# Compression with its weights stationary, and full-width groups for the recurrence's operands, in a two-layer RWKV-7 / sparse-attention trunk

## The chip, the core and the metric

The kernel runs on one core of a Trainium2 chip. Five engines work side by side, each through its own queue in order: TensorE (matmuls and transposes into PSUM), VectorE, ScalarE, GpSimd and SyncE, which issues the DMAs. The metric is the device time of one execution in microseconds.

## The reference

Two layers over 256 tokens of width 2048, batch 1. Each modulates its input, projects it, mixes tokens in two head groups, projects back, normalizes, and applies a squared-ReLU MLP. Two parts of the token mixer matter here.

The recurrence (16 heads of 64) is a generalized delta rule:

```
S = S * w_t[:, :, None, :] + sa[..., None] * (kk_t * a_t)[:, :, None, :] + v_t[..., None] * k_t[:, :, None, :]
return S, jnp.einsum('bhvk,bhk->bhv', S, r_t)
...
o = ((o - mu_o) * lax.rsqrt(var_o + GN_EPS)).reshape(B, T, D_RWKV) * lnx_g + lnx_b
```

The output is centred per head before it is scaled; the kernel centres the values `v` beforehand, which gives the same.

The sparse attention (16 query heads, 4 key/value heads) compresses keys and values: blocks of 32 tokens, every 16 tokens, 15 blocks in all, are flattened to 2048 numbers and put through a small MLP with 256 hidden units.

```
blocks = jnp.transpose(blocks, (0, 3, 1, 2, 4)).reshape(B, G, n_cmp, CMP_BLOCK * N)
return jax.nn.gelu(blocks @ w1) @ w2
```

## The kernel before

Activations lie transposed, features on partitions and the 256 tokens along the free dimension. Every large product is done in three matmuls of a reduced float32 type: the weights arrive by DMA into `wf` (5 buffers, shared with the compression's weights), ScalarE casts them to `wh` (line 226), VectorE makes the remainder `wl` (227), and `mm3` runs `wh*xh + wl*xh + wh*xl` into `acc` (128 stationary columns, 256 moving). `block` does one 128-column output so; its evict step follows. The order on each engine is made by a planner that walks the program with priorities and a cost model, and places other ready work where an instruction would wait. So projection matmuls `acc` stand between the small ones.

The recurrence works on chunks of 64 tokens. `rwkv_a` prepares one pair of heads, 8 pairs in a layer, in two halves of four (`half_in`); it is called 16 times. It makes decay products, normalized keys and, in `bk` (128 partitions = 2 heads x 64 features; 4 chunks x 3 slots x 64 tokens), the scaled operands: slot 0 and 1 for both, and slot 2, a copy of slot 0 for the second head. The matrices `mt` come from `bk` and `UR`; VectorE masks them (543, 544), ScalarE copies parts of them out (547, 549). Then, for each head, four transposes per call turn 64 rows by 128 columns of `bk` into `bkt`, and ScalarE copies `bkt` to `BK` (552 to 555). The centred values: four matmuls take 64 tokens each of `vt` as stationary against the constant `cent` into `vp`, and two ScalarE copies store them in `SV`, the second head on partitions 0 to 63 and the first on 64 to 127 (556 to 560). `bonus` (562) follows. All of `zw`, `za`, `tp`, `rb`, `mt`, `bkt`, `vp` and `bonus` take turns in the two PSUM banks named "a". `rwkv_b` inverts triangular matrices on VectorE, 31 dependent steps in lines 575 and 577; `rwkv_c` runs the chunks one after the other.

`compress` runs twice in a layer (keys, values), after the second and the fourth of the `Kd` projections. `kcp` holds the gathered blocks: 128 partitions, 16 slices of 64 columns (4 heads x 16 blocks). The hidden layer is 16 matmuls with a slice of `kcp` stationary (64 columns) and 256 weight columns moving; they write partitions 0 to 63 and 64 to 127 of `hid` in turn, two partial sums that lines 772 and 773 add. GELU follows on 64 partitions x 256, then two transposes `xt` (781) and a copy bring the hidden units onto partitions for the second layer. The weights come in four DMAs of 512 KB.

In the profile a float32 matmul leaves two records, a transpose one. Nearly all matmuls go through the helper in line 206, so groups are told apart by their tiles.

Of the kernel before, what the change touches and what calls it, by code (L numbers as in the profile page):

```python
# [15 lines left out]
OP = mybir.AluOpType  # L16
# [151 lines left out]
def tile_trunk(tc, ap, outT, dbg=None):  # L168
    nc = tc.nc
    V, A, G, PE, SY = nc.vector, nc.scalar, nc.gpsimd, nc.tensor, nc.sync  # L170
    with ExitStack() as ctx:
# [6 lines left out]
        def st(tag, shape, dt=FT, name=None):  # L178
            if dbg is not None:
                dbg.setdefault("_sz", {})  # L180
                dbg["_sz"][tag] = max(dbg["_sz"].get(tag, 0), int(np.prod(shape[1:])) * 4 * BUFS.get(tag, 1))
            return sb.tile(shape, dt, name=name or tag, tag=tag, bufs=BUFS.get(tag, 1))
# [4 lines left out]
        def mx(th, shape, name="mx"):  # L187
            return psp.tile(shape, FT, name=name, tag="mx" + th, bufs=1 if th in "mn" else 2)
# [10 lines left out]
        ident = cs("ident")  # L199
# [210 lines left out]
        for l in range(NL):  # L410
# [80 lines left out]
            def rwkv_a(pi, p, r, k, H):  # L491
# [48 lines left out]
                for h, (me, ot) in enumerate(halves):  # L540
                    ur, tm, mt = H["UR"][p][h], H["TM"][p][h], mts[h]
                    rm = cs("rmask")
                    V.tensor_mul(ur[ot], mt[ot], rm[ot, None, :].to_broadcast([64, 4, 128]))
                    V.tensor_mul(tm[me, :, 64:128], mt[me, :, 64:128], rm[me, None, 64:128].to_broadcast([64, 4, 64]))
                    for q in range(2):
                        r0 = h * 64 + q * 32
                        A.copy(Dt[r0:r0 + 32, :, p * 4:p * 4 + 4].rearrange("p t c -> p c t"),
                               mt[r0:r0 + 32, :, q * 32:q * 32 + 32])
                    A.copy(tm[h * 64:h * 64 + 32, :, 32:64], mt[h * 64:h * 64 + 32, :, 32:64])
                    tp = mx("a", [128, 4, 64], "bkt")  # L550
                    for c in range(4):
                        PE.transpose(tp[:, c], bk[me, c, h:h + 2].rearrange("p a b -> p (a b)"), ident[me, me])
                    bt = st("BK", [128, 4, 64])
                    H["BK"][p][h] = bt
                    A.copy(bt, tp)
                vp = mx("a", [64, 4, 2, 64], "vp")
                for c in range(4):
                    mm(vp[:, c].rearrange("p a b -> p (a b)"), vt[:, c * 64:c * 64 + 64], cs("cent"))
                A.copy(H["SV"][0][64:128, p], vp[:, :, 0])
                A.copy(H["SV"][1][0:64, p], vp[:, :, 1])  # L560
                bp = mx("a", [128, T], "bonus")
                mm(bp, cs("bones"), sq)
                V.tensor_mul(vt, bp, vt)
# [196 lines left out]

            def compress(kv, kcp):

                hid = mx("n", [128, 256], "hid")
                for q in range(4):
                    w = st("wf", [128, 4, 256], name="cw1")
                    SY.dma_start(w, ap["cw1"][l, kv, q].rearrange("p (a b) -> p a b", a=4))
                    for j in range(4):
                        o = j % 2 * 64
                        mm(hid[o:o + 64], kcp[:, 4 * q + j].rearrange("p g c -> p (g c)"), w[:, j], q * 4 + j < 2, q * 4 + j > 13)
                xr, y = slab(name="xr"), slab(name="gy")  # L770
                xr, y = xr[0:64], y[0:64]
                A.copy(xr, hid[64:128])
                V.tensor_add(xr, xr, hid[0:64])
                A.activation(y, xr, AF.Square)
                V.tensor_scalar(y, y, 0.044715, 1.0, op0=OP.mult, op1=OP.add)
                V.tensor_mul(y, y, xr)
                A.activation(y, y, AF.Tanh, scale=math.sqrt(2.0 / math.pi))
                V.scalar_tensor_tensor(xr, y, 1.0, xr, op0=OP.add, op1=OP.mult)
                xt = mx("n", [128, 2, 64], "xt")
                for b in range(2):  # L780
                    PE.transpose(xt[:, b], xr[:, b * 128:b * 128 + 128], ident[0:64, 0:64])
                x = st("cg1", [128, 2, 64])
                A.copy(x, xt)
                if kv == 0:
                    kp = mx("n", [128, 2, 16], "kp")
                    for g in range(4):
                        for b in range(2):
                            mm(kp[g % 2 * 64:g % 2 * 64 + 64, g // 2], cw2[:, 0, b], x[:, b, g * 16:g * 16 + 16], b == 0, b == 1)
                    for h in range(2):
                        A.mul(kcd[h * 64:h * 64 + 64, :, h], kp[h * 64:h * 64 + 64], 0.5)  # L790
                else:
                    vp = mx("n", [32, 2, 64], "vp2")
                    for gp in range(2):
                        for b in range(2):
                            mm(vp[:, gp], x[:, b, gp * 32:gp * 32 + 32], cw2[:, 1, b], b == 0, b == 1)
                    for h in range(2):
                        A.activation(vcb[:, :, h * 64:h * 64 + 64], vp, AF.Copy, scale=cs("hm")[0:32, h:h + 1])

            Kd = [[None] * 2 for _ in range(2)]
            kcp = compress_in(0)  # L800
# [354 lines left out]
```

## Time and profile before

| | |
|---|---|
| median of 3 runs | 2805.02 us (2801.45 to 2806.73) |
| profiled execution | 2805.57 us, of which the span is 2803.7 us |
| TensorE matmuls | busy 2682.2 us (96%), 22794 records |
| VectorE | busy 2088.5 us (74%) |
| ScalarE | busy 1507.1 us (54%) |
| mean granted TensorE clock | 0.981 of full speed |

The sum of a change is set against the profiled execution. A busy TensorE is not one at its peak: a row's duration holds the time in the pipeline, and neighbouring rows overlap. Where the matmuls are packed, the distance between starts tells what one costs.

### The profile page before, as it was taken

Reading aid. Unit: us, or ns where it says so; the run is one execution under the profiler, and the core shown is the slowest. Engines: PE = TensorE matmul, PEld = TensorE weight load, DVE = VectorE, ACT = ScalarE, POOL = GpSimd, SP = SyncE. Lnnn points to the kernel's source line nnn. Section 1 sums busy time; section 2 is a strip of 40 time slices with the busy share of each in tenths; the row PEclk is TensorE's granted clock in tenths of the full one; section 3 lists DMA queues with packets and bytes.
Section 4 is the critical chain, followed back from the end, with each engine's and each line's share of the span. In section 5 each row is a group of like instructions: output and inputs, shape, how many; then the busy total and the mean of one; then the engine's idle time right before and its main releaser. Section 6 shows DMA issues by size and latency. Waiting matters only on the chain.

```text
span 2803.7 us, 59395 instructions
## 1 busy us (share of the span) xinstructions
PE 2682.2 (96%) x22794; PEld 2450.1 (87%) x22794; DVE 2088.5 (74%) x4710; ACT 1507.1 (54%) x3221; POOL 69.6 (2%) x205
## 2 busy tenths in 40 slices
PE   6999899998999999999999999999999999999997
PEld 4777678756999999999999888887799999999997
DVE  3677868656789788888998786886796566666567
ACT  3344345554585554645557544556567565464555
POOL 0000010000000000000000001000000000000000
PEclk9999999898999999999999999999999999999998
DMA  8986656386579899999986444333466777776664
GB/s 302 320 271 229 239 190 196 121 265 211 171 231 370 316 344 339 338 352 336 342 266 200 140 150 129 120 107 119 157 197 187 235 217 235 231 233 205 195 191 126
DMA packets 206780, 639.63 MB, mean 228 GB/s; under 512 B 23392, under 2 KB 42848, under 8 KB 206496
## 3 DMA queue, kind: packets, MB, share of 16 engines
q1 hardware_dynamic: 206496, 635.83, 68.0%
q8 instruction: 179, 2.93, 0.4%
q14 instruction: 105, 0.86, 0.1%
HBM read 629.45 MB, written 6.29 MB: 227 GB/s over the span
## 4 chain that ended last, share of the span: by engine, by line
PE 78%; DVE 13%; DMA 4%; ACT 3%; issue 2%; SPq 0%; ACTq 0%; POOL 0%; DVEq 0%
PE acc L206 65%; DVE wl L227 4%; PE gv L206 2%; DMA wap<-in_wad 1%; ACT wh L226 1%; PE ot L206 1%; PE pt L896 1%; PE mt L206 1%; DMA wf<-in_win 1%; DVE Tt L577 1%; DVE fs L575 1%; PE va L206 1%; PE vp L206 1%; PE tp L206 0%; PE rb L206 0%
## 5 line engine op out<-in xcount | busy, mean ns | idle before, releaser
L226 ACT CAST wh<-wf 128x512 fp32r<-128x512 f32 x1536 | 946.1, 620 | 859.0 <-PE acc L206 483.4
L227 DVE TENSOR_TENSOR wl<-wf,wh 128x512 fp32r<-128x512 f32 x1536 | 1038.5, 689 | 384.2 <-ACT wh L226 372.8
L206 PE MATMUL acc<-hhi,wh 128*128 128x256 f32 x3456 | 983.5, 285 | 17.1 <-ACT wh L226 8.8
L206 PE MATMUL acc<-hhi,wl 128*128 128x256 f32 x3456 | 972.3, 281 | 8.7 <-DVE wl L227 8.5
L206 PE MATMUL acc<-hlo,wh 128*128 128x256 f32 x3456 | 971.9, 282 | 0.2 <-DVE hlo L407 0.2
L206 PE MATMUL acc<-hi,wh 128*128 128x256 f32 x2560 | 714.8, 279 | 8.1 <-DVE res L1059 3.8
L206 PE MATMUL acc<-lo,wh 128*128 128x256 f32 x2560 | 715.4, 280 | 1.3 <-DVE lo L215 1.3
L206 PE MATMUL acc<-hi,wl 128*128 128x256 f32 x2560 | 714.8, 279 | 0.1
L206 PEld LDWEIGHTS acc<-hhi,wh 128*128 128x128 f32 x3456 | 656.8, 190 | 61.2 <-issue 24.1
L206 PEld LDWEIGHTS acc<-hhi,wl 128*128 128x128 f32 x3456 | 655.7, 190 | 18.2 <-DVE wl L227 12.9
L206 PEld LDWEIGHTS acc<-hlo,wh 128*128 128x128 f32 x3456 | 654.6, 190 | 8.7 <-issue 4.5
L206 PEld LDWEIGHTS acc<-hi,wh 128*128 128x128 f32 x2560 | 484.6, 189 | 10.5 <-ACT hi L214 5.0
L206 PEld LDWEIGHTS acc<-lo,wh 128*128 128x128 f32 x2560 | 483.3, 189 | 3.6 <-DVE lo L215 2.4
L206 PEld LDWEIGHTS acc<-hi,wl 128*128 128x128 f32 x2560 | 484.1, 189 | 1.4 <-issue 0.8
L344 DVE CUSTOM_DVE_ANT_0 wa<-wa,cond,modh 128x1024 f32<-128x1024 f32 x112 | 143.3, 1279 | 0.0
L344 DVE CUSTOM_DVE_ANT_0 wa<-wa,cond,vec 128x1024 f32<-128x1024 f32 x112 | 143.3, 1279 | 0.0
L206 PE MATMUL gv<-wap,cT 128*32 128x512 f32 x640 | 90.6, 639 | 21.7 <-DMA wap<-in_wad 21.4
L1099 DVE TENSOR_TENSOR lo<-relu,hi 128x256 fp32r<-128x256 f32 x128 | 54.1, 425 | 45.5 <-ACT relu L1098 45.3
L288 DVE TENSOR_TENSOR sum<-sum,acc 128x512 f32<-128x512 f32 x70 | 48.1, 687 | 45.8 <-PE acc L206 45.8
L883 ACT ACTIVATE P<-P,tyn 128x128 f32<-128x128 f32 (+1 forms) x128 | 57.3, 448 | 11.8 <-DVE tyn L881 11.1
L1097 ACT ACTIVATE hi<-relu 128x256 fp32r<-128x256 f32 x128 | 53.5, 422 | 3.5
L1098 ACT ACTIVATE relu<-relu 128x256 f32<-128x256 f32 x128 | 53.3, 420 | 3.6
(290 smaller groups left out, 2352.5 us busy)
## 6 DMA issues: line engine op xcount, KB each, us to landing
wf<-in_w SPq DMA_DIRECT2D x512, 512.0 KB, 4.6
wa<-in_wada SPq DMA_DIRECT2D x224, 512.0 KB, 5.6
wf<-in_win SPq DMA_DIRECT2D x192, 512.0 KB, 4.1
wap<-in_wad SPq DMA_DIRECT2D x208, 256.0 KB, 4.7
wf<-in_wout SPq DMA_DIRECT2D x64, 512.0 KB, 4.1
wap<-in_wad SPq DMA_DIRECT2D x56, 512.0 KB, 5.1
cw<-in_cw SPq DMA_DIRECT2D x16, 512.0 KB, 4.1
xin<-in_xT SPq DMA_DIRECT2D x16, 128.0 KB, 5.5
```

What stands on the lines that cost most here:

```text
L206: return PE.matmul(o, l, r, start=start, stop=stop, skip_group_check=True)
L226: A.copy(wh, wf[:, s])
L227: V.tensor_sub(wl, wf[:, s], wh.bitcast(FT))
L288: V.tensor_add(s, s, bank)
L344: V.tensor_tensor_reduce(wa, wa, cb, 0.5, init, OP.mult, OP.add, dst)
L575: V.tensor_mul(x, Mu[:, j + 1:32, j:j + 1].to_broadcast([128, n, w]), Tt[:, j:j + 1, 0:w].to_broadcast([128, n, w]))
L577: V.tensor_sub(Tt[:, j + 1:32, 0:w], Tt[:, j + 1:32, 0:w], x)
L883: A.activation(P[:, h, c:c + n], P[:, h, c:c + n], AF.Exp, bias=m[:, 2 * h + i:2 * h + i + 1], scale=-1.0, accum_out=z[:, 2 * h + i:2 * h ...
L896: PE.transpose(pt[:, h, c * 128:c * 128 + 128], P[:, h, 256 * i + c * 128:256 * i + c * 128 + 128], ident)
L1097: A.activation(hi, t, AF.Square)
L1098: A.activation(t, t, AF.Square)
L1099: gate[0] = V.tensor_sub(lo, t, hi.bitcast(FT)).ins
```

## The change

Three edits. In `rwkv_a`, the two groups of four transposes with 64 rows become one group of four with all 128 rows, both heads at once; the first head's operand is copied out in one piece, the second's in two, with the halves of the partitions exchanged (slot 2 is still made for `mt`). The centred values take 128 tokens a matmul, two matmuls instead of four, and four copies of 64x128 in place of two of 64x256. In `compress` the weights become stationary (128 columns) and the 64 columns of `kcp` move; the hidden units so land on partitions, the two partial sums and their addition, the two transposes and one copy go, and GELU works on 128 partitions x 128.

```diff
-                    tp = mx("a", [128, 4, 64], "bkt")
-                    for c in range(4):
-                        PE.transpose(tp[:, c], bk[me, c, h:h + 2].rearrange("p a b -> p (a b)"), ident[me, me])
-                    bt = st("BK", [128, 4, 64])
-                    H["BK"][p][h] = bt
-                    A.copy(bt, tp)
-                vp = mx("a", [64, 4, 2, 64], "vp")
+                tp = mx("a", [128, 4, 128], "bkt")
                 for c in range(4):
-                    mm(vp[:, c].rearrange("p a b -> p (a b)"), vt[:, c * 64:c * 64 + 64], cs("cent"))
-                A.copy(H["SV"][0][64:128, p], vp[:, :, 0])
-                A.copy(H["SV"][1][0:64, p], vp[:, :, 1])
+                    PE.transpose(tp[:, c], bk[:, c, 0:2].rearrange("p a b -> p (a b)"), ident)
+                H["BK"][p] = [st("BK", [128, 4, 64]) for h in range(2)]
+                A.copy(H["BK"][p][0], tp[:, :, 0:64])
+                for r in (0, 64):
+                    A.copy(H["BK"][p][1][64 - r:128 - r], tp[r:r + 64, :, 64:128])
+
+                vp = mx("a", [128, 2, 2, 64], "vp")
+                for i in range(2):
+                    mm(vp[:, i].rearrange("p a b -> p (a b)"), vt[:, i * 128:i * 128 + 128], cs("cent"))
+                for e in range(2):
+                    for h in range(2):
+                        A.copy(H["SV"][h][64 - h * 64:128 - h * 64, p, e:4:2], vp[e * 64:e * 64 + 64, :, h])
...
-                hid = mx("n", [128, 256], "hid")
+                hid = mx("n", [128, 2, 64], "hid")
...
-                        o = j % 2 * 64
-                        mm(hid[o:o + 64], kcp[:, 4 * q + j].rearrange("p g c -> p (g c)"), w[:, j], q * 4 + j < 2, q * 4 + j > 13)
-                xr, y = slab(name="xr"), slab(name="gy")
-                xr, y = xr[0:64], y[0:64]
-                A.copy(xr, hid[64:128])
-                V.tensor_add(xr, xr, hid[0:64])
+                        for b in range(2):
+                            mm(hid[:, b], w[:, j, b * 128:b * 128 + 128], kcp[:, 4 * q + j].rearrange("p g c -> p (g c)"),
+                               q + j + b == 0, q * 4 + j == 15)
+                xr, y = slab(name="xr")[:, 0:128], slab(name="gy")[:, 0:128]
+                x = st("cg1", [128, 2, 64])
+                A.copy(xr, hid.rearrange("p a b -> p (a b)"))
...
-                V.scalar_tensor_tensor(xr, y, 1.0, xr, op0=OP.add, op1=OP.mult)
-                xt = mx("n", [128, 2, 64], "xt")
-                for b in range(2):
-                    PE.transpose(xt[:, b], xr[:, b * 128:b * 128 + 128], ident[0:64, 0:64])
-                x = st("cg1", [128, 2, 64])
-                A.copy(x, xt)
+                V.scalar_tensor_tensor(x.rearrange("p a b -> p (a b)"), y, 1.0, xr, op0=OP.add, op1=OP.mult)
```

## Rows read from the trace of the kernel before

**Rows 1.** The page's part 4: chain that ended last, shares by engine.
```profile
PE 78%; DVE 13%; DMA 4%; ACT 3%; issue 2%; SPq 0%; ACTq 0%; POOL 0%; DVEq 0%
```
**Rows 2.** Busy time by stretch: length, PE, PEld, DVE, ACT, POOL, clock, DMA share, GB/s.
```profile
1610.00:1630.00 20.00, 19.61 (x151) 17.61 (x150) 15.87 (x48) 11.96 (x27) 0.70 (x4) 1.00 0.36 111
1650.00:1670.00 20.00, 18.71 (x154) 17.61 (x152) 19.22 (x49) 6.58 (x13) 0.00 (x0) 1.00 0.49 158
```
**Rows 3.** TensorE's waits over the span: us in total, times, longest.
```profile
PE bkt L552 <- ACT TM L549: 2.9, 9, 0.6
...
PE hid L206 <- DMA cw<-in_cw: 2.1, 3, 1.6
```
**Rows 4.** Timeline of TensorE, one call in layer 1: start, us, what (stationary, moving).
```profile
1620.24 0.28 PE L206 MATMUL acc<-hlo,wh 128*128 128x256 f32 x1
1620.45 0.46 PE L552 MATMUL bkt<-cst,a 64*128 64x64 f32 x4
...
1621.07 0.28 PE L206 MATMUL acc<-hhi,wl 128*128 128x256 f32 x1
...
1622.35 0.28 PE L206 MATMUL acc<-hhi,wl 128*128 128x256 f32 x1
1622.47 0.28 PE L206 MATMUL acc<-hlo,wh 128*128 128x256 f32 x1
1622.68 1.09 PE L206 MATMUL vp<-cst,vt 128*64 128x128 f32 x8
1623.70 0.39 PE L206 MATMUL acc<-hhi,wh 128*128 128x256 f32 x1
1623.92 0.28 PE L206 MATMUL acc<-hhi,wl 128*128 128x256 f32 x1
1624.04 0.59 PE L206 MATMUL bonus<-a,cst 128*128 128x256 f32 x2
...
1624.69 0.48 PE L206 MATMUL zw<-lx,wa 96*128 96x256 f32 x1
```
**Rows 5.** Timeline of TensorE around four transposes of 128 by 128.
```profile
422.72 0.28 PE L206 MATMUL acc<-hlo,wh 128*128 128x256 f32 x1
422.84 0.60 PE L385 MATMUL gv<-cst,gs 128*128 128x128 f32 x4
423.19 0.37 PE L206 MATMUL acc<-hhi,wh 128*128 128x256 f32 x1
423.40 0.28 PE L206 MATMUL acc<-hhi,wl 128*128 128x256 f32 x1
```
**Rows 6.** Timeline of TensorE: float32 matmuls with 128 stationary columns.
```profile
212.32 0.52 PE L206 MATMUL tp<-cst,a 128*128 128x2 f32 x4
212.71 0.36 PE L206 MATMUL acc<-hhi,wh 128*128 128x256 f32 x1
...
403.17 1.06 PE L206 MATMUL rb<-lx,g 128*128 128x256 f32 x4
```
**Rows 7.** Groups of ScalarE by form: busy us, mean ns of one, idle before.
```profile
L555 ACT COPY BK<-bkt 128x256 f32<-128x256 f32 x32 | 11.8, 373 | 5.0 <-PE bkt L552 4.7
L549 ACT COPY TM<-mt 32x128 f32<-32x128 f32 x32 | 8.2, 256 | 0.5
L560 ACT COPY SV<-vp 64x256 f32<-64x256 f32 x16 | 5.9, 367 | 0.2
```
**Rows 8.** Timeline of ScalarE in the call of rows 4.
```profile
1624.27 0.37 ACT L560 COPY SV<-vp 64x256 f32<-64x256 f32 x1
```
**Rows 9.** Timeline of TensorE: the compression's `hid` matmuls, three of their runs.
```profile
314.59 1.08 PE L206 MATMUL hid<-cw,kcp 128*64 128x256 f32 x8 [1.55 <-DMA cw<-in_cw]
...
1671.92 4.92 PE L206 MATMUL hid<-cw,kcp 128*64 128x256 f32 x26
...
1693.15 3.64 PE L206 MATMUL hid<-cw,kcp 128*64 128x256 f32 x30 [1.02 <-DVE fs L575]
```
**Rows 10.** Busy time by stretch, columns as in rows 2.
```profile
1672.00:1676.00 4.00, 4.00 (x24) 2.33 (x25) 3.34 (x10) 0.43 (x1) 0.00 (x0) 0.58 0.70 245
```

## The prediction

> **What bounds the kernel now.** I read the chain that ended last first: TensorE's matmuls hold 78% of it, VectorE 13%, transfers 4% [rows 1]. So a microsecond of TensorE time is, on average, most of a microsecond of the result. Then the busy time in the stretches of the change: in the first half of layer 1's recurrence TensorE is busy for 19.61 of 20 us, VectorE for 15.87, ScalarE for 11.96; forty microseconds later, while the triangular inverse runs, VectorE has 19.22 and TensorE 18.71 [rows 2]. TensorE is the limit while the operands are made, and two engines are close to it during the compression. Last come TensorE's waits: all transposes `bkt` together waited 2.9 us for ScalarE, and `hid` 2.1 us for its weights [rows 3]. Little is lost in waiting around the edited lines, so what must be counted is how long each matmul group occupies the array. That isn't the duration of a row, since matmuls overlap; it is the distance from the start of one row to the start of the next.
>
> **Transposes of the recurrence's operands.** In the run of projection matmuls, starts are 0.12 us apart (1622.35 to 1622.47). A group of four `bkt` transposes, 64 rows by 128 columns, takes from 1620.24 to 1621.07, 0.83 us with two ordinary steps of 0.12 in it, so 0.59 us; 0.09 of that is on entry (0.21 to its first row instead of 0.12) [rows 4]. There are two groups in each call: 1.18 us. The new group is four transposes of 128 by 128. The trace has just that at `gv`: 422.72 to 423.40 is 0.68, less 0.24, so 0.44 us; entry costs nothing extra there [rows 5]. Gain: 0.74 us a call.
>
> **Centred values.** Eight `vp` records (each float32 matmul leaves two) take 1622.47 to 1623.92, which is 1.45 less 0.24, so 1.21 us, and 1.02 from their start to the next row's, 0.128 a record [rows 4]. Four records with the same 128 moving columns but 128 stationary ones replace them. They are bounded by `tp`, whose records have 128 stationary and 2 moving columns and stand 0.39 / 4 = 0.098 us apart, and by 0.128; full-width records with 256 moving columns last 1.06 us for four (`rb`) and 0.59 for two (`bonus`), 0.235 each, so half as many columns take 0.118 [rows 4, 6]. I take 0.11, between `tp` and `rb`; the 0.128 has a switch in it. So 0.44, and 0.09 for entry and exit as at `gv`: 0.53. Gain 0.68 us, with bounds 0.61 and 0.73. With the transposes it is 1.42 us a call, and there are 16 calls (8 head pairs, 2 layers): **-22.7 us**.
>
> **ScalarE's copies.** `BK` for the second head becomes two copies of 64 partitions instead of one of 128: 0.373 + 2 x 0.367 instead of 2 x 0.373, so +0.36 us. `SV` becomes four copies of 64x128 for two of 64x256. The trace has no 64x128 copy; it lies between 0.256 (32x128) and 0.367 (64x256) [rows 7]. I take 0.256, as the elements along a partition are the same: +0.29 (at most +0.73). Together +0.65 us a call, 10.4 us of ScalarE. What hides it is the 8 us in 20 that ScalarE is idle [rows 2], and projection matmuls that the planner puts between. What it delays is the next call: its first matmul `zw` starts at 1624.69 [rows 4], just after the last `SV` copy, 1624.27 plus 0.37 [rows 8], since `zw` and `vp` draw on the same two banks. Behind a late `zw` in TensorE's queue stand the projection matmuls. Nothing lost in most calls and the whole 0.65 in some: I charge 0.2 a call, **+3 us** (bounds 0 and 10.4; at the upper `SV` price 17).
>
> **Compression.** Before, 8 records of `hid` last 1.08 us and 30 last 3.64, so 22 more are 2.56 us, 0.116 each [rows 9]; 32 make 3.7, and 0.2 for entering and leaving: 3.9 us. After, there are 64 records: 128 stationary columns are loaded for 64 moving ones. Load and moving part overlap in the rows seen, so the load sets the pace: 0.098 (`tp`) to 0.128 (`vp`) [rows 6, 4]. I take 0.11: 7.0 us, +0.1: 7.1, so +3.2. The two `xt` transposes go; by the `bkt` group, 0.59 less two of its four records, some 0.45 us. Net +2.75, four times: **+11.0 us** (bounds +8 and +15). Of this the `hid` matmuls' waits for weights are given back, as a slower group waits less: one quarter of the weights was waited for 1.55 us [rows 9], all together 2.1 [rows 3]. **-2 us**. One VectorE addition, one ScalarE copy less and shorter operations between also fall away, off TensorE; I take nothing for them, though where VectorE is full [rows 2] they may be worth 1 or 2 us. The DMAs are the same 16 transfers in the same place; each buffer is held some 0.8 us longer, which delays the next weight load where transfers are the limit.
>
> The pairs of `hid` now write two 64-column strips of the array, and their 256 columns cost 0.116 us where an `rb` record of 256 costs 0.235 [rows 9, 6]. So the two run side by side, and the edit gives that up. The Trainium skill, TensorEngine Tiling (Array Packing), section When to Use Tiling, advises just the form that is taken away: with 64 or fewer moving columns, swap the operands and tile the columns by two. By that rule alone the edit doubles the compression's array time; by the rows it nearly does, and it is the other two edits that would have to pay for it.
>
> **Sum.** -22.7 + 3 + 11 - 2 = -10.7 us. The profiled execution took 2805.57 us, 0.55 above the median of the runs shown; the sum gives 2794.9, and from the median 2794.3. I forecast 2794 us, its own range 2786 to 2799. A measurement of this kernel can tell about 0.2%, 5.6 us, from no change.
>
> **Rivals.**
> *The freed TensorE time is not the limit.* The projection matmuls that move up need `wl` from VectorE, which is full from 1650 on [rows 2]. If only half of the -22.7 is kept, the sum is -11.3 + 3 + 9, about +1: 2806, no change. For it speaks the nearness of VectorE; against it, the first half, where VectorE has 4 us in 20 to spare. Chance 0.17.
>
> *ScalarE's queue sets the pace of the calls (slower).* Place: `zw` behind the last `SV` copy. A call for which this holds gains nothing on TensorE and ends 0.65 us later, instead of 1.42 earlier. With n such calls the sum is -22.7 + 2.07 n + 9: it turns at 7 of 16 and is slower by over 0.2% from 10; with all 16 it is +19, 2825 us. Rows 8 speak for it, the small waits of rows 3 against it. Chance 0.11.
>
> *The clock falls during the compression (slower).* The granted clock is 0.58 on average from 1672 to 1676 us, so it stood at its lower level, 1.2 GHz, for most of that [rows 10], and 26 records of `hid` take 4.92 us there, 0.19 each [rows 9]. In the new form the moving part fills only half the time of each load. At the lower level 64 records cost 14 us, 7 more. Two of four compressions would end at +3, three at +10, 2815 us, and only from there is it slower by over 0.2%. Against it: the 0.58 is no 0.50, so the clock came back while `hid` ran, and the other groups ran at 0.116 a record. Chance 0.08 for three or four.
>
> *Loads don't overlap.* If the load and the moving part followed each other, a record would cost 0.098 and some 0.06 (a quarter of `rb`'s 0.235), 0.158; 64 make 10.1 instead of 7.0, four times +12.4: about +2, 2807, no change. The rows of `rb` speak against it: with loads as wide, their 0.235 is also what two of `hid`'s side by side give (twice 0.116), whose loads are half as wide; a load of 0.098 in series would show. The Trainium skill, TensorE: Matmul & The Clock Gate, Part 3, says that a weight load overlaps a running matmul only where the row groups differ, which would be this case; Part 2 of that page allows it also for the background buffer. By the first rule the time would be this rival's. Chance 0.05.
>
> **Chances.** The forecast and a larger gain 0.59. Faster 0.61 (with 0.02 of the half-kept case); same 0.22 (the rest of that case, the loads, and ScalarE in 7 to 9 calls); slower 0.17 (ScalarE in ten calls or more, the clock). The range: at the lower end -22.7 - 1, no cost of ScalarE, compression at +8 - 2: -18, and another 5 if a stretch at half clock goes; 2782. At the upper end it takes in the cases without change and the milder slow ones (ScalarE in up to 10 or 11 calls): 2811.
>
> **What would show it.** `bkt` with 64 records of 128x128 instead of 128, one group of about 0.44 us a call; `vp` with 64 records instead of 128, 0.45 from start to next; `hid` with 256 records some 0.11 apart, 7 us a time, at clock 1.00; no `xt`; ScalarE's busy time up by 8 us or so; TensorE still busy for over 19 of 20 us in layer 1's first half, with calls closer together than 19 us. I am wrong if `zw` waits for `SV` on TensorE, if `hid` stands at the lower clock, or if the projection matmuls wait longer for `wl`.

## The result and the profile after

The changed kernel took 2821.62 us, median of 8 runs (2811.86 to 2826.31), beside 2803.98 us for the kernel before in the same session. The ratio is 1.0055, 95% interval [1.0032, 1.0077]: slower, by some 15 us, where 2794 us was forecast. Three of the eight runs took 2812 to 2814 us and five 2821 to 2826 us; the profiled one is of the first three (2811.86 us, span 2810.1 us).

The chain that ended last hardly changed; it shows by itself neither the loss nor where it lies [rows 1]:

```profile
PE 78%; DVE 12%; ACT 5%; DMA 3%; issue 2%; SPq 0%; POOL 0%; ACTq 0%; DVEq 0%
```

The sizes that the prediction gave to the groups of matmuls are there. In TensorE's timeline of a call of layer 1 (the columns of [rows 4]) the four transposes take 0.41 us to the next start, and the four `vp` records 0.46 and 0.09 on leaving (0.21 to the second `acc` for 0.12):

```profile
1575.24 0.28 PE L206 MATMUL acc<-hhi,wh 128*128 128x256 f32 x1
1575.78 0.66 PE L552 MATMUL bkt<-cst,a 128*128 128x128 f32 x4 [0.26 <-ACT TM L549]
1576.19 0.36 PE L206 MATMUL acc<-hhi,wl 128*128 128x256 f32 x1
1576.84 0.71 PE L206 MATMUL vp<-cst,vt 128*128 128x128 f32 x4 [0.28 <-ACT TM L549]
1577.30 0.36 PE L206 MATMUL acc<-hlo,wh 128*128 128x256 f32 x1
1577.51 0.28 PE L206 MATMUL acc<-hhi,wh 128*128 128x256 f32 x1
```

But both groups now begin with a wait, in brackets. Of TensorE's waits over the whole span, that of `vp` for `TM` was 0.9 us, 4 times, before; those of `zw` for `SV` and of `bonus` for `BK` are new, and `hid` waits no longer for its weights but for the gather on VectorE [rows 3]:

```profile
PE vp L206 <- ACT TM L549: 4.4, 11, 0.6
PE bkt L552 <- ACT TM L549: 2.1, 7, 0.4
PE hid L206 <- DVE kcp L761: 2.0, 1, 2.0
PE zw L206 <- ACT SV L563: 1.6, 7, 0.4
PE bonus L206 <- ACT BK L556: 1.0, 3, 0.4
```

The windows say the same: TensorE, busy for 19.61 of 20 us before, is busy for 18.95 now [rows 2]. Of the 1.3 us of array time that a call needs less, 0.7 us in these 20 stand there as idle time. From the first `gp` of layer 1 (transposes ahead of its recurrence) to its first `hid`, a stretch with four of the calls, both kernels need 146.1 us (1521.5 to 1667.6 before, 1514.7 to 1660.8 after), and `zw` follows `zw` at 20.0 us where it was 19.1 and 19.7.

```profile
1610.00:1630.00 20.00, 18.95 (x139) 16.91 (x139) 15.33 (x46) 12.53 (x30) 0.72 (x3) 1.00 0.38 112
...
1684.00:1688.00 4.00, 2.93 (x16) 2.77 (x17) 3.16 (x8) 0.00 (x0) 0.00 (x0) 0.75 0.22 35
1688.00:1692.00 4.00, 4.00 (x21) 4.00 (x20) 3.73 (x11) 1.14 (x2) 0.31 (x1) 0.50 0.67 227
1692.00:1696.00 4.00, 4.00 (x21) 4.00 (x20) 1.55 (x3) 0.00 (x0) 0.00 (x0) 0.50 0.44 131
1696.00:1700.00 4.00, 4.00 (x20) 4.00 (x20) 0.00 (x0) 0.66 (x3) 0.00 (x0) 0.50 0.52 139
```

The last four rows are the second compression of layer 1. From the first `hid` to the first `va` the kernel before needed 122.9 us (1667.6 to 1790.5), the changed one 137.5 (1660.8 to 1798.3); `va` belongs to the sparse attention, behind the compression. These 14.6 us are more than the 6.3 us between the two profiled executions, since the changed one had entered layer 1 6.8 us ahead. Most of that lead, 5.8 us, arose behind layer 0's first `va`, where only one of its eight calls lies, at a mean clock of 0.99 for 0.98, so little of it can come from the edits. The two runs of 56 `hid` records in that layer show how:

```profile
1663.75 6.36 PE L206 MATMUL hid<-kcp,cw 128*128 128x64 f32 x56
...
1685.07 1.08 PE L206 MATMUL hid<-kcp,cw 128*128 128x64 f32 x8 [1.96 <-DVE kcp L761]
...
1686.89 12.04 PE L206 MATMUL hid<-kcp,cw 128*128 128x64 f32 x56
```

The first run takes 0.114 us a record, at full clock. The second comes behind a wait of 1.96 us for the gather, and takes 0.215 a record. TensorE is busy for all of 1688 to 1700, and the granted clock is 0.50, the level of 1.2 GHz, all the while. In the kernel before such a run also began slowly, but the clock was back within some 4 us [rows 9, 10], as its window from 1676 us shows (columns as in rows 2):

```profile
1676.00:1680.00 4.00, 4.00 (x34) 3.54 (x31) 3.12 (x7) 1.90 (x5) 0.21 (x1) 0.99 0.98 299
```

In the kernel before, VectorE was busy for 19.22 of 20 us around the start of the first compression [rows 2]. Here it stands still for much of the slow run, as its own timeline shows:

```profile
1692.29 1.26 DVE L227 TENSOR_TENSOR wl<-wf,wh 128x512 fp32r<-128x512 f32 x2
1702.33 0.69 DVE L227 TENSOR_TENSOR wl<-wf,wh 128x512 fp32r<-128x512 f32 x1 [8.78 <-ACT wh L226]
1703.04 1.00 DVE L588 COPY TM<-O 32x128 f32<-32x128 f32 x6
```

A remainder `wl` waits 8.78 us for its cast `wh`. In ScalarE's queue that cast stands behind the copy `xr`, which itself waits for the last `hid`:

```profile
1698.97 0.27 ACT L776 COPY xr<-hid 128x128 f32<-128x128 f32 x1 [8.17 <-PE hid L206]
...
1701.68 0.62 ACT L226 CAST wh<-wf 128x512 fp32r<-128x512 f32 x1 [2.06 <-issue]
```

It starts when twelve projection matmuls behind `hid` have run; that it waits for the buffer that they free is argued, since the trace names no releaser. Behind `wl` in VectorE's queue stands the result of the triangular inverse (`TM<-O`), on which the recurrence's next matmuls hang. So a slow compression is paid for twice, in its own time and in what it holds up.

ScalarE's new copies came out as costed [rows 7], and its busy time is 1516.3 us, 9.2 more:

```profile
L563 ACT COPY SV<-vp 64x128 f32<-64x128 f32 x64 | 16.7, 260 | 1.0
L556 ACT COPY BK<-bkt 64x256 f32<-64x256 f32 x32 | 11.7, 367 | 0.4
```

### The profile page after: what moved, and what is told of

Its sections match the earlier page's. It is cut to its first block, busy times and chain, and to the rows that moved or that the text cites. A ratio compares the mean times of both kernels' runs of the same rounds, so it can differ in the third digit from the quotient of the medians.

```text
span 2810.1 us, 59434 instructions
## 1 busy us (share of the span) xinstructions
PE 2684.2 (96%) x22786; PEld 2466.5 (88%) x22786; DVE 2088.4 (74%) x4706; ACT 1516.3 (54%) x3265; POOL 71.2 (3%) x205
## 4 chain that ended last, share of the span: by engine, by line
PE 78%; DVE 12%; ACT 5%; DMA 3%; issue 2%; SPq 0%; POOL 0%; ACTq 0%; DVEq 0%
PE acc L206 65%; DVE wl L227 4%; PE gv L206 2%; ACT wh L226 1%; PE hid L206 1%; PE ot L206 1%; DMA wap<-in_wad 1%; PE pt L894 1%; PE mt L206 1%; ACT Dt L547 1%; PE va L206 1%; PE tp L206 1%; PE sc L206 1%; DVE Tt L580 0%; DVE fs L578 0%
## 5 line engine op out<-in xcount | busy, mean ns | idle before, releaser
L881 ACT ACTIVATE P<-P,tyn 128x128 f32<-128x128 f32 (+1 forms) x128 | 57.3, 448 | 13.8 <-DVE tyn L879 12.5
```

What stands on the lines that cost most here:

```text
L881: A.activation(P[:, h, c:c + n], P[:, h, c:c + n], AF.Exp, bias=m[:, 2 * h + i:2 * h + i + 1], scale=-1.0, accum_out=z[:, 2 * h + i:2 * h ...
```

## The experiments

In the table a ratio is to the kernel before, run on the same chip; clock is the mean granted clock over all executions of a kernel, beside that of the kernel before in the same session. A straight line through the 265 executions, each kernel about its own mean, gives 1.5 us for each 0.001 of clock. "Rest" is the difference of the means less that much: it is a rough guide, good to perhaps 3 us.

| kernel | median us | ratio, 95% | clock (before) | rest us |
|---|---|---|---|---|
| recur_only | 2796.34 | 0.9988 [0.9971, 1.0004] | 0.9793 (0.9794) | -4 |
| compress_only | 2816.86 | 1.0060 [1.0042, 1.0077] | 0.9775 (0.9794) | +13 |
| more_scalar | 2801.73 | 1.0000 [0.9987, 1.0013] | 0.9793 (0.9794) | +1 |
| wide_moving | 2800.89 | 1.0010 [0.9994, 1.0025] | 0.9831 (0.9799) | +8 |
| two_kcp | 2821.08 | 1.0077 [1.0051, 1.0102] | 0.9758 (0.9799) | +15 |
| layer0_only | 2805.03 | 1.0022 [1.0005, 1.0038] | 0.9805 (0.9799) | +6 |
| layer1_only | 2816.46 | 1.0050 [1.0031, 1.0070] | 0.9773 (0.9805) | +9 |
| recur_wide | 2806.52 | 1.0050 [1.0032, 1.0068] | 0.9810 (0.9816) | +11 |
| recur_vector | 2797.49 | 0.9997 [0.9982, 1.0013] | 0.9797 (0.9799) | -1 |
| half_array | 2790.85 | 0.9983 [0.9969, 0.9997] | 0.9802 (0.9816) | -7 |
| before_short | 2794.58 | 0.9990 [0.9975, 1.0004] | 0.9802 (0.9816) | -5 |
| recur_short | 2785.51 | 0.9966 [0.9953, 0.9978] | 0.9799 (0.9816) | -13 |
| half_short | 2783.95 | 0.9945 [0.9930, 0.9960] | 0.9812 (0.9805) | -15 |
| recur_two | 2784.06 | 0.9941 [0.9925, 0.9958] | 0.9827 (0.9805) | -13 |
| before_two | 2803.94 | 1.0022 [1.0005, 1.0038] | 0.9767 (0.9803) | 0 |
| recur_two_b | 2784.80 | 0.9957 [0.9942, 0.9972] | 0.9811 (0.9803) | -13 |

The changed kernel itself has a mean clock of 0.9749.

### Which edit

**recur_only**: the two edits of the recurrence, with the compression as before.

> The two recurrence edits without the compression's. If TensorE's array time sets the pace of the calls (my sum), this is 20 to 23 us faster than before, less some 3: about 2785 us. If the chain of a call through ScalarE sets it, the freed array time is worth nothing and each of the 16 calls ends 0 to 0.65 us later: 0 to +10 us, 2804 to 2814, and zw starts stand 19.7 to 20.3 us apart in the first half of layer 1 instead of 19.1 to 19.7.

**compress_only**: the compression's edit, with the recurrence as before.

> The compression's edit without the recurrence's. If only array time counts, +9 to +11 us, about 2814. If the clock falls in layer 1's second compression as it does in the changed kernel, and VectorE's queue stands behind the longer hid, +12 to +25 us, and hid's records are 0.21 us apart there. If recurrence edits and compression only hurt together, under +5 us.

**more_scalar**: the kernel before, with the copies `SV` made twice.

```diff
-                A.copy(H["SV"][0][64:128, p], vp[:, :, 0])
-                A.copy(H["SV"][1][0:64, p], vp[:, :, 1])
+                for _ in range(2):
+                    A.copy(H["SV"][0][64:128, p], vp[:, :, 0])
+                    A.copy(H["SV"][1][0:64, p], vp[:, :, 1])
```

> The kernel before with its two SV copies made twice, so 0.73 us more of ScalarE in each of 16 calls and nothing else. If ScalarE's queue sets the pace of the calls, most of 16 x 0.73 = 11.7 us is seen: +6 to +12 us, and zw starts stand 0.5 to 0.7 us further apart. If TensorE sets it and ScalarE's idle time covers the copies: 0 to +2 us.

**after_again**: the changed kernel once more.

> The changed kernel unaltered, for a second profile. Its times lie at 2812 to 2814 us and at 2819 to 2826. If the clock makes that difference, this profile has the same order of work and other stretches at the lower clock, 10 us or more of it in a run of the upper group; if one stretch is always cold, it is hid of layer 1's second compression in both.

The loss is the compression's: 1.0060 alone. The recurrence's edits alone gained 3 us of the 20 that the prediction gave them (8 gained to 1 lost by the interval), which is between the two outcomes that were expected. By the differences of the means, -4 and +16 add up to 12 of the changed kernel's 15 us. ScalarE's added volume is not the reason: 0.73 us a call more of it, in the kernel before, cost nothing that can be measured. after_again took 2826.1 us, with most of both compressions of layer 1 at a clock of 0.50, where the profiled run of the changed kernel had one. That explains only a part of the 14 us between the two: from the first `hid` of layer 1 to the first `va` it needed 142.7 us for 137.5, so 5 us; 4 more were lost between layer 0's first `va` and layer 1's first `gp`, and 5.5 behind layer 1's first `va`. Only these two executions were seen in a trace.

### The compression: clock, queue or array time

**wide_moving**: compress_only with the moving columns streamed twice.

```diff
-                            mm(hid[:, b], w[:, j, b * 128:b * 128 + 128], kcp[:, 4 * q + j].rearrange("p g c -> p (g c)"),
+                            mm(hid[:, b], w[:, j, b * 128:b * 128 + 128], kcp[:, 4 * q + j].rearrange("p g c -> p (g c)")[:, None, :].to_broadcast([128, 2, 64]),
```

> The compression's part of the change alone, with every moving part of its products streamed twice (128 columns instead of 64; the second half of the result is not used). Theory (clock): compression alone cost 0.6% because layer 1's products, with their short moving part, run at a granted clock of 0.50 from their first to their last record and no longer bring the clock back; with twice the columns TensorE is kept busier for each weight load, and if that is what the clock answers to, the granted clock in layer 1's compressions returns to 1.00 within a few us, and the kernel takes 2800 to 2810 us, ratio 1.000 to 1.004. Rival A (the weight loads alone set the pace and the clock, the moving part is indifferent): the records stay at 0.21 us each at half clock, ratio 1.006 as without the edit. Rival B (the queue of VectorE behind the single gather buffer is the cost): ratio 1.006 or more, since the products get longer, 0.21 us to 0.25 us a record.

**two_kcp**: compress_only with two gather buffers (`"S": 51` for 52, and `"QN": 2`).

> The compression's part of the change alone, with two buffers for the gathered blocks, so that VectorE can gather the values' blocks while TensorE still reads the keys' (one other work buffer of 52 given up for it). Rival B (VectorE's queue stands behind the gather, and with it the triangular inverse of the next call): the wait of VectorE on TensorE's products in layer 1 (2.58 us in the changed kernel) disappears, the half-clock stretches get shorter, ratio 0.999 to 1.003. Theory (clock): the gather was late because the products were slow, not the other way round; the wait disappears but the products of layer 1 still run at half clock, ratio 1.004 to 1.007.

**layer0_only** and **layer1_only**: the compression's edit under `if l == 0` or `if l == 1`, the other layer as before.

> The compression's part of the change in layer 0 alone; layer 1 computes as before. Theory: layer 0's products run at full clock in every trace so far, and the loss lies between 1660 and 1718 us in layer 1: ratio 0.997 to 1.002, milestones of layer 1 as in the kernel before. Rival: the loss is the 2.75 us of added array time per compression plus queue effects in both layers alike: ratio 1.003, half of the 1.006 of both layers.

> The compression's edit in layer 1 alone. Both layers together cost 0.60%, layer 0 alone 0.22%. If the loss is two equal shares of array time and a share for the clock in layer 1, ratio 1.0035 to 1.0050; if layer 1's loss hangs on what layer 0 did before it, under 1.003.

The gather's queue falls as a cause. In the trace of compress_only VectorE's gather waited for the products of `hid` for 8.4 us at a stretch; in that of two_kcp no such row is left, and the kernel is no faster. The split by layer says that there are two costs. Layer 0 loses 5 to 6 us with no loss of clock: this is the array time that the prediction had at 2.75 us a compression. Layer 1 loses 14, with a clock 0.0032 lower. layer0_only's ratio lies just outside what was expected if layer 0 costs nothing (0.997 to 1.002) and nearer to its rival's 1.003; the interval covers some of both.

wide_moving costs next to nothing; by the line through the clocks that is because its clock is 0.0032 higher than that of the kernel before, and the array time is still paid (rest +8). How one slow start goes on shows in TensorE's timeline in layer 1, first layer1_only with 64 moving columns, behind a wait of 2.77 us:

```profile
1671.93 1.22 PE L206 MATMUL acc<-rx,cst 128*128 128x256 f32 x2 [2.77 <-ACT rx L728]
1672.94 12.05 PE L206 MATMUL hid<-kcp,cw 128*128 128x64 f32 x56
```

and then wide_moving with 128, behind a wait of 2.60 us, where 58 records need 4 us less than those 56, though each streams twice as much:

```profile
1662.11 0.70 PE L206 MATMUL acc<-rx,cst 128*128 128x256 f32 x2 [2.60 <-ACT rx L728]
1662.65 8.27 PE L206 MATMUL hid<-kcp,cw 128*128 128x128 f32 x58
```

In wide_moving's second compression of layer 1 the planner spread the products among others, so that run alone doesn't show what the form does. **clock_forms** measures it by itself, behind the last result of the kernel before:

```diff
+                for form in ("narrow", "wide", "pair", "narrow", "wide", "pair"):
+                    for i in range(24):
+                        mm(full, ident, base, i == 0, i == 23)
+                    V.tensor_copy(base, full)
+                    for i in range(8):
+                        V.tensor_scalar(base, base, 1.0, None, op0=OP.mult)
...
+                            mm(h[o:o + 64], sta[i // 2 % 2][:, o:o + 64], base, i < 2, i > 61)
...
+                            mm(h, sta[i % 2], x[:, None, :].to_broadcast([128, 2, 64]), i == 0, i == 63)
...
+                            mm(r, sta[i % 2], x, i == 0, i == 63)
```

> The kernel before, and behind its last result a measurement that adds nothing to it: six times, TensorE first runs 24 full products of 256 columns, then stands idle for some 3 us while VectorE copies, then runs 64 products (128 records) of one of three forms: 128 columns loaded and 64 moving (the changed compression), 128 loaded and 128 moving (the widened one), 64 loaded and 256 moving in pairs (the compression before), in this order, twice. Theory: after the idle stretch all three start or soon fall to a granted clock of 0.50; the pairs come back to 1.00 within some 4 us, as in the kernel before, while the narrow form stays at 0.50 to its last record (128 records in about 27 us), and the wide one comes back. Rival (the form is indifferent, and what the clock does depends on the idle time alone): all three come back after the same time, 128 records of the narrow form in 14 to 17 us.

TensorE's timeline there, one row for each run of 128 records:

```profile
2857.42 14.56 PE L206 MATMUL wide<-base,cst 128*128 128x128 f32 x128 [3.14 <-DVE base L1154]
...
2886.16 15.72 PE L206 MATMUL pair<-base,cst 128*64 128x256 f32 x128 [3.23 <-DVE base L1154]
...
2916.06 26.58 PE L206 MATMUL narrow<-base,cst 128*128 128x64 f32 x128 [3.23 <-DVE base L1154]
...
2959.12 17.30 PE L206 MATMUL wide<-base,cst 128*128 128x128 f32 x128 [3.14 <-DVE base L1154]
```

and the windows of the narrow run and of the second wide one (length, PE, clock, DMA share, GB/s):

```profile
2916.00:2920.00 4.00, 3.94 (x23) 0.64 0.02 4
2920.00:2924.00 4.00, 4.00 (x21) 0.50 0.00 0
...
2936.00:2940.00 4.00, 4.00 (x21) 0.50 0.00 0
...
2960.00:2964.00 4.00, 4.00 (x21) 0.50 0.01 2
2964.00:2968.00 4.00, 4.00 (x34) 0.89 0.00 0
2968.00:2972.00 4.00, 4.00 (x38) 1.00 0.00 0
```

After the same idle 3.2 us the narrow form fell to 0.50 and stayed there to its last record, 0.21 us each; its other run, at 2816, did the same. The wide form and the pairs each fell in one of their two runs; the wide form was back at 1.00 within 8 us, the pairs within some 6. That is one execution, but the kernels' traces agree: all six narrow runs of 56 records that met the low clock kept it to their end (12.05 us in compress_only, two_kcp and layer1_only, 12.04 in the changed kernel, 10.53 and 11.83 in after_again), and the runs at full clock (6.36 us) kept theirs. At full clock the wide form takes 14.56 / 128 = 0.114 us a record, the price of the narrow one: with 64 moving columns the load sets the pace, and streaming half as much saves nothing. The Trainium skill, TensorE: Matmul & The Clock Gate, Part 1, says that the throttled state is the default and that activity releases it. The rows add that a TensorE which the profile shows busy for 4.00 of 4 us, window after window, can stay at 0.50.

**recur_wide**: the changed kernel with the wide form.

> The changed kernel whole, with every moving part of the compression's products streamed twice (128 columns instead of 64, the second half of the result unused). Theory (clock): as with the compression's edit alone, the clock comes back within a few us in each compression, some 15 to 20 us are regained, ratio 0.998 to 1.002 against the kernel before. Rival (the recurrence's and the compression's edits collide in layer 1 in another way than by the clock): ratio stays over 1.004.

It failed: 1.0050, hardly better than the changed kernel's 1.0055, though the mean clock was back (0.9810, for 0.9816 before). The parts by the table are +8 (wide_moving's rest) and -4, and +1 for its clock: some +5, where the means differ by 12. So wide_moving's 1.0010 owed much to a clock better than that of the kernel before, which this kernel didn't have; about 7 us of the difference stay unexplained. Its trace shows where they may lie: from the first `hid` of layer 1 to the first `va` it needs 133.8 us (122.9 in the kernel before). In the second compression the planner put the wide products among the recurrence's small ones, and there the clock stayed low (windows as for clock_forms):

```profile
1688.00:1692.00 4.00, 4.00 (x56) 0.50 0.32 90
1692.00:1696.00 4.00, 4.00 (x41) 0.50 0.45 184
1696.00:1700.00 4.00, 4.00 (x49) 0.50 0.02 4
```

So the wide form brought the clock back where it ran by itself, and not in this mixture.

### The recurrence: where 20 us went

**recur_vector**: recur_only with half of the `SV` copies on VectorE.

```diff
-                        A.copy(H["SV"][h][64 - h * 64:128 - h * 64, p, e:4:2], vp[e * 64:e * 64 + 64, :, h])
+                        (A.copy if e == 0 else V.tensor_copy)(H["SV"][h][64 - h * 64:128 - h * 64, p, e:4:2], vp[e * 64:e * 64 + 64, :, h])
```

> The recurrence's part of the change alone, with two of the four copies of centred values moved from ScalarE to VectorE. Theory (the array time saved in a call was given back by ScalarE's chain between the eviction of the transposes and the state product zw): the chain gets shorter by two copies of 0.26 us, zw in layer 1 follows at 19.4 to 19.7 us instead of 20.0, and the kernel is 5 to 10 us faster than with the recurrence's edits alone, ratio 0.995 to 0.998. Rival (the pace of calls is set by the rest of TensorE's work and VectorE's queue, not by ScalarE's copies): zw at 20.0 as before, ratio 0.998 to 1.002.

**half_array**: the kernel before with half of both groups left out (`twice` repeats two chunks by a broadcast).

```diff
-                    for c in range(4):
+                    for c in range(2):
                         PE.transpose(tp[:, c], bk[me, c, h:h + 2].rearrange("p a b -> p (a b)"), ident[me, me])
...
-                    A.copy(bt, tp)
+                    A.copy(two(bt), twice(tp[:, 0:2]))
-                for c in range(4):
+                for c in range(2):
                     mm(vp[:, c].rearrange("p a b -> p (a b)"), vt[:, c * 64:c * 64 + 64], cs("cent"))
```

> The kernel before with half of the transposes bkt and half of the centring products vp left out; ScalarE's copies read the same amount (each transposed chunk twice, by a broadcast), so its work is unchanged, and the outputs of two of four chunks are those of the other two. TensorE's array time for the two groups falls from 1.80 us a call, as measured in the kernel before, to about 0.9, the same as with the recurrence's edits (0.87). Theory (a call's length is set by the chain of dependent steps through VectorE and ScalarE, so freed array time turns into waits): ratio 0.998 to 1.002, zw in layer 1 19 to 20 us apart as before. Rival (ScalarE's added copies ate a gain that was there): with no added copies 0.9 us x 16 calls = 15 us are kept, ratio 0.993 to 0.996.

**before_short** and **recur_short**: one step of Newton's iteration in the reciprocal root of a call, in the kernel before and in recur_only; **half_short** is half_array with it.

```diff
-            rsqrt(y, v, t)
+            rsqrt(y, v, t, 1)
```

> The kernel before with the same four operations of the reciprocal root dropped per step, that is one step of Newton's iteration instead of three. Theory: TensorE is idle for only 2.6 of 90 us in layer 1's first half here, so a shorter chain can give at most 0.6 us a call, 10 us in all: ratio 0.997 to 1.000, less than the same edit gives with the recurrence's edits in. Rival (the chain through VectorE sets the pace in both kernels alike): both gain the same, ratio 0.990 to 0.994 here too.

> The recurrence's edits alone, with one step of Newton's iteration instead of three in the reciprocal root of a call (six VectorE operations of 128x4, some 0.15 us each, left out; that root is then coarser). Theory (the chain through VectorE between tp and rb sets the calls' length): each call gets shorter by 0.9 us and by the remainders wl that stand between those six, and now TensorE's saved 0.93 us is kept too: ratio 0.987 to 0.994, zw in layer 1 18 to 19 us apart. Rival (TensorE's total work or the order that the planner chose sets the pace): ratio 0.997 to 1.000, zw at 20 us.

> The kernel before with half of bkt and vp left out as in half_array, and with one step of Newton's iteration instead of three. If the chain through VectorE is what kept half_array from keeping its 15 us, both together give much more than the sum of each alone (0.17% and 0.10%): ratio 0.992 to 0.995. If each gives its own little share, ratio 0.996 to 0.9985.

half_array takes away 0.9 us a call, 15 us, and adds no copy, and it keeps 5 (1 to 9 by the interval). So most of the gain is lost even with ScalarE's work as it was. It and recur_only lie 1 to 3 us apart, less than their intervals, so the price of the added copies is not resolved. recur_vector's fewer copies on ScalarE brought nothing, and `zw` still came every 20.2 us; since the copies went to VectorE, whose result `exa` was then waited for longer (2.1 us in four calls, 0.7 in recur_only), it doesn't test ScalarE alone. recur_short, at 0.9966, lies between its theory and its rival.

TensorE's waits from 1570 to 1650, some four calls of layer 1, show who holds it there. In the kernel before, all of them:

```profile
PE rb L308 <- DVE exa L305: 1.3, 4, 0.4
PE bkt L552 <- ACT TM L549: 0.8, 3, 0.3
PE vp L206 <- ACT TM L549: 0.3, 1, 0.3
```

in half_array, all of them:

```profile
PE rb L308 <- DVE exa L305: 1.9, 4, 0.7
PE mt L206 <- DVE UR L535: 0.7, 2, 0.5
PE bonus L206 <- ACT TM L549: 0.5, 2, 0.3
PE bkt L552 <- ACT TM L549: 0.3, 1, 0.3
PE vp L206 <- ACT TM L549: 0.2, 1, 0.2
```

in half_short, all of them:

```profile
PE bkt L552 <- ACT TM L549: 0.2, 1, 0.2
```

The wait for `exa` is the end of a chain on VectorE: `tp`, then eleven operations for the root, between which VectorE's queue also runs the remainders `wl` for the projection. Freed array time brings TensorE earlier to the end of that chain: of some 3.6 us freed in these four calls, 1.2 come back as longer waits and 1.2 are kept (144.9 us from `gp` to `hid`, for 146.1); the last third isn't seen in the waits. With the chain shorter too the waits are gone, TensorE is busy for 19.73 us from 1590 to 1610, `zw` follows at 18.4 us, 142.9 us pass from `gp` to `hid`, and half_short keeps 15 us of the kernel. Its two edits taken singly give 8 by the ratios, but 12 by the column of rests, which hardly tells 12 from 15. In recur_only the waits are spread over both engines (`vp` for `TM` 1.1, `bkt` for `TM` 0.9, `rb` for `exa` 0.7, `mt` for `UR` 0.6); recur_short takes away those for VectorE, and `vp` then waits 2.1 us for ScalarE's `TM`.

### A version that beats both

**recur_two**: recur_only with two steps, `rsqrt(y, v, t, 2)`; **before_two**, its control: the kernel before with two steps; **recur_two_b**: recur_two again, beside it.

> The recurrence's edits alone with two steps of Newton's iteration instead of three, which leaves the root accurate to some 5e-6: a version meant to beat both kernels. By recur_only (0.9988) and recur_short (0.9966, one step): ratio 0.9970 to 0.9985 if each step counts the same; 0.9988 or more if only the last of the two steps taken away in recur_short counted.

> The kernel before with two steps of Newton's iteration instead of three, the control for recur_two (0.9941). If the shorter chain pays only where TensorE's work in a call is shorter too: ratio 0.998 to 1.000, as with one step (0.999). If the iteration's step alone made recur_two faster: 0.993 to 0.996.

> The recurrence's edits with two steps of Newton's iteration, once more, on the same chip as its control. By its first run: ratio 0.9925 to 0.9958.

recur_two is 12 to 16 us faster than the kernel before, and by the ratios some 27 to 32 faster than the changed one. The control is not faster: 1.0022, outside both ranges given for it, at a clock lower by 0.0036, and with a rest of 0. By the rests the recurrence's edits give 4 us, the two steps nothing and both together 13, twice: more than the sum, and clear of that column's precision. Of recur_two's first ratio some 3 us are a higher clock; even so it came out faster than either expectation had it. That it is the chain which lets the array time be kept is argued for this version: in layer 1 `zw` still follows at 19.1 and 20.0 us, and most of the gain in the traces lies in layer 0 and behind it (from the first `gp` to the first `va` 238.6 us before, 235.7 in recur_only, 239.4 in before_two, 229.9 and 230.7 in recur_two and recur_two_b). That one step (recur_short) gave no more than two was not expected; with each edit the planner also orders the queues anew, and what part of these few us is its order was not separated.

## Why the prediction was wrong

**Array time of the recurrence: right.** The groups took 0.41 and 0.46 us to the next start, with 0.09 on leaving (seen at `vp`) 0.50 and 0.55; forecast were 0.44 and 0.53. About 1.3 us a call are freed (2.39 - 1.05); 1.42 were forecast.

**That freed array time is kept: wrong.** This is the first step that failed: "Little is lost in waiting around the edited lines, so what must be counted is how long each matmul group occupies the array." The forecast took small waits to mean that operands were ready with time to spare. The runs showed otherwise: half_array kept 5 of 15 us, recur_only 4 of 20. The waits that grew in their place are for the root's chain on VectorE and for ScalarE's copies; they cover a part of what was lost, and the rest of it was not traced. The rival that the freed time is not the limit was the right one for this edit, at 0.17, but with the wrong cause: `wl` was not waited for longer by the projection (7.0 us in all, 8.5 before); the small matmuls waited for their operands. The 4 us in 20 that VectorE has to spare, named against it, say nothing of a chain.

**ScalarE's copies: not contradicted.** +3 us were charged; more_scalar, with 11.7 us more of ScalarE's work, cost between -4 and +4. The rival in which its queue sets the pace did not come: `zw` waited for `SV` only 1.6 us in all.

**Compression's array time: right.** Forecast +11 us, with bounds of +8 and +15; the rest in compress_only is +13, in layer0_only +6 for half of it. A record took 0.114 us at full clock (0.11 forecast), and 64 of them in one run 7.25 to 7.41 us in layer 0 (7.1 forecast). So loads don't stand in series with the moving part, and the rival of serial loads (0.158 a record) falls. The Trainium skill, TensorE: Matmul & The Clock Gate, has both rules; the row fits that of Part 2 (the background buffer), not that of Part 3 (only with different row groups).

**Given back in waits for weights: wrong, 2 us.** The wait for `cw` is gone, and one of 2.0 us for `kcp` stands in its place.

**The clock: the mechanism was named, and its weight was wrong.** The rival priced a slow compression rightly: 14 us for 64 records, 13.8 measured (64 x 0.215). But it counted whole compressions and needed three for a loss, and it got 0.08 for three or four because "the clock came back while `hid` ran". That was read from the old form, pairs of 256 columns. clock_forms and the kernels' traces show that it doesn't hold for the new one: none of eight narrow runs that met the low clock came back before its last record. This is the second step that failed, a property of a form carried over to the form that replaces it. No three slow compressions were needed for a loss, since the recurrence did not pay for the array time as assumed. What the clock costs the changed kernel is not settled: by its mean, 0.9749 against 0.979 to 0.982, 6 to 10 us of the 15; by recur_wide, which has the mean clock back, 1 to 4.

**The sum as measured:** -4 (recurrence) + 16 (compression, with its clock) = 12, for -19.7 + 9 as forecast; both together measured 15. So 16 us were missed at the first step, 7 at the compression, and 3 lie within the noise or in what the two do to each other. The Trainium skill's rule in TensorEngine Tiling (Array Packing), When to Use Tiling, which spoke against this edit, was right: what it advises was the faster form, by 16 us in compress_only.

## What to carry to other kernels

Before a saved microsecond on the busiest engine is counted, ask which operand its next instruction will then wait for: an engine that is 98% busy with short waits can be in balance with a chain, and shortening both can pay where either alone hardly does. Where matmuls with a load of 128 columns and 64 moving ones follow an idle stretch, as here, reckon with the slow clock for all of them; streaming 128 columns for each load cost nothing more, and where such products ran by themselves the clock returned. And price an edit from rows of the form that it brings in, not of the one that it takes out.

## What the runs showed of the hardware

- 64 and 128 moving float32 columns behind a load of 128 columns cost the same at full clock, 0.114 us a record (6.36 / 56 and 14.56 / 128).
- At full busy time in the profile, 4.00 of 4 us, the narrow form (64 moving columns) kept TensorE at a granted clock of 0.50 for over 20 us; 128 moving columns or pairs of 256, run by themselves, brought it to 1.00 within 8 us. Mixed with the recurrence's small products (recur_wide), 128 columns left it at 0.50 from 1688 to 1700.
- 0.001 of mean clock went with 1.5 us of time over 265 executions, about half of the 2.8 us (an estimate: 0.001 of 2800) that it would be if every such stretch lay on the path.
